# A hybrid encoder block in fp32: gate and value as one loop over both halves of the tokens, operands loaded later in program order, made operands in the ring of the sums

## The chip, the cores and the metric

One core of one Trainium2 chip. The time is the device time of one execution in microseconds (us); lower is better. TensorE is PE in the profile (its weight loads PEld), VectorE is DVE, ScalarE is ACT, GpSimd is POOL, SyncE is SP. SPq and ACTq are the DMA issues in the instruction streams of SP and ACT.

## The reference

One layer on 2048 tokens of width 1024 with a feed-forward width of 2816. Everything is fp32. The change lies in `conv_ffn`.

```python
def reference(x, ...):
    h = rmsnorm(x, mix_norm_w[i])
    y = gla_mixer(h, gla_w_in, gla_w_gate2, gla_b_gate, gla_norm_w, gla_w_out)
    x = x + y
    h = rmsnorm(x, ffn_norm_w[i])
    x = x + conv_ffn(h, w_up, conv_w, conv_b, w_down)
    return rmsnorm(x, final_norm_w)

def conv_ffn(h, w_up, conv_w, conv_b, w_down):
    u = causal_dwconv(h @ w_up, conv_w, conv_b)   # 3 taps along the tokens
    g, val = jnp.split(u, 2, axis=-1)
    return (jax.nn.silu(g) * val) @ w_down
```

## The kernel before, in words

The mixer's projections run as four passes (R, A, B, Y). The feed-forward then has two parts: gate and value (`phase_u`, h @ w_up with convolution, Silu and product) and down (w_down). A fp32 product is made of three matmuls on split numbers: `split` writes a rounded copy (ACT, the CAST of L184) and the rest (DVE, the TENSOR_TENSOR of L185).

**Products.** Each large matrix product is done by a seven-product scheme on 2 by 2 blocks: `OPS` names the seven products p1, p5, p6, p7, p4, p2, p3 in the order in which they run. A product is 12 matmuls of 128x512 (4 slices of the inner dimension, 3 matmuls each, L177 to L179) into a PSUM bank. p1, p6, p7 and p4 add up in one bank (`ua`), p5 and p3 in another (`uc`), p2 has its own (`ub`). Between them ACT copies the bank out: after p1 (c1, L1052), after p6 (c2, L1052), after p7 (c3, L1143) and after p4 (L1150). The next product into that bank has to wait for the copy.

**Gate and value before.** `phase_u(s)` runs once for each half s of the tokens (1024 each). In it 22 column blocks f go in 11 groups of two; a group is 14 products (seven for each of its two f). In each half there are therefore 154 products. For each group:
- `load` brings raw blocks of w_up (`ur`, 256 KB a DMA, on SP) into a ring of four; those for the next group are asked for at products 2 and 7 of this one.
- `prep` makes and splits the weight operand of a product (`uw_p`), five products ahead (`ULEAD`); POOL makes the sums (`us`).
- `conv` and `gated` turn u into the gated product t; POOL makes four sums of it (`as_p`, a ring of four 2 KB tiles that c3 shares), and SP stores them to DRAM (`ad_p<-as_p`) with the products themselves (`ad_p<-t`).

**Operands of the tokens.** The token side of each of the seven products stays in SBUF for a whole half (`h_p`, 2 MB each, tile `uh`). It is made once by `prep_h2` (split into `h2p_p`), stored to DRAM (`hd_p`), and brought back by `load_op` in four DMAs of 512 KB on SP. For the second half the 28 operands (7 products times 4 pairs of token tiles) are made while the first half of gate and value runs: `spread` calls one step about every 11 us of planned PE time; it loads rows (`h2r`) on SP, subtracts (L791), splits, and stores through ACT's queue (L786). Before, the tile `h2p` for this has a single buffer of 4 KB a partition (hi and lo together) in the pool `wx`.

**What sets the order.** The instructions of each engine run in the order of the program. That order comes from the order of the calls, from the planned clock (`later_do` delays a call by a planned time), and from a scheduler that moves instructions ahead on an engine where it takes them to be ready. An engine, SP and ACT as DMA issuers too, stops at the first instruction that must wait.

**Between the halves before.** The loop of s = 0 ends; only then does `phase_u(1)` ask for its first raw blocks and make its first weights. The seven `load_op` of the second half stand right behind the last use of the same operand of the first half.

**Last tiles of h.** `x1_done` normalises a tile of 128 tokens, and `blocks` transposes it on PE (`pt_d`, L755) NLY = 5.5 us of planned time later. For the last two tiles (14, 15) this falls among the first products of gate and value.

Of the kernel before, what the change touches and what calls it, by code (L numbers as in the profile page):

```python
# [16 lines left out]
P = 128  # L17
# [8 lines left out]
def hybrid_kernel(  # L26
# [36 lines left out]
    WB = 4  # L63
    WX = 3
    HB = 4
    RB = 4
# [3 lines left out]
    DLY, KLY, XLY = 5.0, 2.0, 6.5  # L70
    NLY = 5.5
    Y0, Y1, U0, U1 = 3.0, 2.8, 14.0, 11.0
# [667 lines left out]
    def x1_done(t, xt):  # L740
        if "p" not in yp:
            y_open()
        (nc.scalar if t + 2 >= NTT else nc.sync).dma_start(x1d[t], xt)
        rws = yp["p"].tile([P, D], F32, tag="rows", name=f"h2_{t}", bufs=2)
        rstd = rstd_of(xt, D, f"d{t}", rws, "a")
        nc.scalar.activation(rws, xt, AF.Identity, scale=rstd)
        later_do(NLY, lambda: blocks(t, rws))

# [20 lines left out]
    def prep_h2(jj, raw, pair):  # L769
# [13 lines left out]
        def store():  # L783
            while held:
                o, hl = held.pop()
                (nc.scalar if s else nc.sync).dma_start(hd[s, o, j], f32(hl))  # L786
# [77 lines left out]
    def unit(ps_, j):  # L864
# [28 lines left out]
        for i, o in enumerate(PORD):  # L893
# [31 lines left out]
            if j + 1 == NP:  # L925
                if nxt:
                    if i == 0:
                        plan_w(nxt)
                else:
                    if i == 0:  # L930
                        need(*(f"h2p{jj}" for jj in range(PAIRS)))
                    load_op(0, o)
                    if i == 3:
                        ux["u"] = phase_u(0)
                        next(ux["u"])
# [72 lines left out]

    def phase_u(s):
        raws, wops, sums, made = {}, {}, {}, {}  # L1010
        jobs = [(g, o, f) for g in range(NQ) for o in OPS for f in (2 * g, 2 * g + 1)]


        def load(g, n):
            for f in (2 * g, 2 * g + 1):
# [6 lines left out]
        def prep(k):  # L1022
            g, o, f = jobs[k]
            a11, a21 = raws[f, 0][:, 0, :], raws[f, 0][:, 1, :]
# [29 lines left out]

        def new_u(i, f):
            c = f + i * NF
# [4 lines left out]

        def conv(i, f):
            c = f + i * NF
# [10 lines left out]

        def gated(f):
            t, v = made.pop(("t", 0, f)), made.pop(("t", 1, f))
# [26 lines left out]
        bank = {}  # L1103
        for k, (g, o, f) in enumerate(jobs):
            if k % (2 * len(OPS)) in (2, 7) and g + 1 < NQ:
                load(g + 1, int(k % (2 * len(OPS)) == 7))
            if s == 0 and k == 6:
                while delayed:
# [3 lines left out]
                pools["us"] = pools["ctx"].enter_context(tc.tile_pool(name="us", bufs=1, reuse_waits="tile"))  # L1112
                pools["wx"] = wx_ = pools["ctx"].enter_context(tc.tile_pool(name="wx", bufs=1, reuse_waits="tile"))
                spread(range(PAIRS, 2 * PAIRS), U0, U1, row_tile,
                       lambda name: wx_.tile([P, 2, 512], F32R, tag="h2p", name=name, bufs=1))
            if s == NS - 1 and g == NQ - 1 and f % 2 == 0:
# [17 lines left out]
            elif o == "p2":  # L1134
                pb = mm_ps(f"ub_{s}_{f}")
                mm3p(pb, pairs)
                ev, _ = new_u(0, f)
                nc.vector.tensor_add(ev, tiles1(pb), tiles1(made.pop(("p1", f))))
            elif o == "p7":
                a = bank["a", f]  # L1140
                mm3p(a, pairs, first=False, more=True)
                u3 = pools["us"].tile([P, 512], F32, tag="as", name=f"c3_{s}_{f}", bufs=4)
                nc.scalar.copy(u3, a)  # L1143
                ev, od = new_u(1, f)
                made["ev", f] = ev
                nc.vector.tensor_add(od, tiles1(bank["c", f]), tiles1(u3))
            elif o == "p4":
                a = bank.pop(("a", f))
                mm3p(a, pairs, first=False, more=True)
                nc.scalar.copy(made.pop(("ev", f)), tiles1(a))  # L1150
                conv(1, f)
# [6 lines left out]
            if o == "p3":  # L1158
                _, od = tiles2(made["u", 0, f][:, 2:2 + TS])
                nc.vector.tensor_add(od, tiles1(c), tiles1(made.pop(("u2", f))))  # L1160
                conv(0, f)
                gated(f)

# [232 lines left out]
```

## Time and profile before

| | |
|---|---|
| median of 3 runs | 2259.55 us (2251.75 to 2259.7) |
| the profiled execution: time, span | 2255.93 us, 2254.2 us |
| gate and value, first half (11 groups) | 909.81 to 1373.58 us of the span |
| gate and value, second half (11 groups) | 1373.58 to 1822.53 us |
| PE busy over the span | 2125.4 us, 94% |
| DVE, ACT, POOL busy | 71%, 49%, 32% |

In the views a row of the timeline is: start, duration, engine, line, operation, out<-in, shape, count, and in brackets the idle time of the engine just before it with what ended it. A row of a table of stretches is: from:to, length, then busy time and number of instructions of PE, PEld, DVE, ACT and POOL, the granted TensorE clock (1.00 is full), the DMA share and GB/s.

### The profile page before, as it was taken

Reading aid. Unit: us, or ns where it says so; the run is one execution under the profiler, and the core shown is the slowest. Engines: PE = TensorE matmul, PEld = TensorE weight load, DVE = VectorE, ACT = ScalarE, POOL = GpSimd, SP = SyncE. Lnnn points to the kernel's source line nnn. Section 1 sums busy time; section 2 is a strip of 40 time slices with the busy share of each in tenths; the row PEclk is TensorE's granted clock in tenths of the full one; section 3 lists DMA queues with packets and bytes.
Section 4 is the critical chain, followed back from the end, with each engine's and each line's share of the span. In section 5 each row is a group of like instructions: output and inputs, shape, how many; then the busy total and the mean of one; then the engine's idle time right before and its main releaser. Section 6 shows DMA issues by size and latency. Waiting matters only on the chain.

```text
span 2254.2 us, 29125 instructions
## 1 busy us (share of the span) xinstructions
PE 2125.4 (94%) x9948; PEld 1738.4 (77%) x9948; DVE 1609.5 (71%) x2175; ACT 1111.0 (49%) x2020; POOL 712.1 (32%) x602
## 2 busy tenths in 40 slices
PE   5999989989998999989999996999999999999998
PEld 4788778877886787767777884888888887888886
DVE  7755787788778675488898774786767776557464
ACT  4554655565556676444554452554544543232342
POOL 1000111111111000355555663555555534036100
PEclk9999999999999999999999997999999999999999
DMA  6545683368557799935544248324242468354443
GB/s 209 197 165 180 209 289 122 122 213 314 164 159 235 250 328 337 334 126 191 178 145 146 83 126 308 108 80 131 71 138 72 131 239 309 129 188 153 140 168 117
DMA packets 301045, 411.77 MB, mean 183 GB/s; under 512 B 23246, under 2 KB 159614, under 8 KB 300896
## 3 DMA queue, kind: packets, MB, share of 16 engines
q1 hardware_dynamic: 266156, 346.72, 46.1%
q10 hardware_dynamic: 34740, 63.19, 8.2%
q8 instruction: 78, 1.28, 0.2%
q14 instruction: 71, 0.58, 0.1%
HBM read 266.70 MB, written 143.13 MB: 182 GB/s over the span
## 4 chain that ended last, share of the span: by engine, by line
PE 67%; DVE 12%; DMA 9%; issue 5%; ACT 4%; POOL 3%; ACTq 0%; SPq 0%; DVEq 0%; POOLq 0%
PE ua L177 5%; PE ua L178 5%; PE ua L179 5%; PE pd_p L178 5%; PE pd_p L177 5%; PE pd_p L179 5%; PE uc L178 3%; PE uc L179 3%; PE uc L177 3%; DVE t L1070 2%; PE mp_R L177 2%; PE mp_R L178 2%; PE mp_R L179 2%; PE mp_Y L177 2%; PE mp_Y L178 2%
## 5 line engine op out<-in xcount | busy, mean ns | idle before, releaser
L177 PE MATMUL ua<-h_p,uw_p 128*128 128x512 f32 x704 | 281.2, 399 | 45.3 <-ACT uw_p L184 22.0
L178 PE MATMUL ua<-h_p,uw_p 128*128 128x512 f32 x704 | 279.2, 397 | 0.0
L179 PE MATMUL ua<-h_p,uw_p 128*128 128x512 f32 x704 | 278.5, 396 | 0.0
L1070 DVE SCALAR_TENSOR_TENSOR t<-u,cw,t 128x1024 f32<-128x1024 f32 x176 | 249.9, 1424 | 11.2 <-ACT t L1068 9.7
L178 PE MATMUL pd_p<-dw_p,da 128*128 128x512 f32 x616 | 240.5, 390 | 1.9 <-DVE da L185 1.9
L177 PE MATMUL pd_p<-dw_p,da 128*128 128x512 f32 x616 | 240.4, 390 | 0.0
L179 PE MATMUL pd_p<-dw_p,da 128*128 128x512 f32 x616 | 240.3, 390 | 0.0
L185 DVE TENSOR_TENSOR uw_p<-ur,uw_p 128x512 fp32r<-128x512 f32 x176 | 159.4, 920 | 84.7 <-ACT uw_p L184 71.2
L185 DVE TENSOR_TENSOR da<-da_p,da 128x512 fp32r<-128x512 f32 x154 | 131.9, 910 | 102.3 <-ACT da L184 102.2
L177 PEld LDWEIGHTS ua<-h_p,uw_p 128*128 128x128 f32 x704 | 134.2, 191 | 81.3 <-ACT c L1052 26.5
L184 ACT CAST da<-da_p 128x512 fp32r<-128x512 f32 x154 | 85.1, 619 | 204.5 <-PE pd_p L179 148.7
L185 DVE TENSOR_TENSOR uw_p<-us,uw_p 128x512 fp32r<-128x512 f32 x132 | 119.1, 910 | 63.3 <-ACT uw_p L184 56.5
L179 PEld LDWEIGHTS ua<-h_p,uw_p 128*128 128x128 f32 x704 | 134.3, 191 | 30.1
L178 PEld LDWEIGHTS ua<-h_p,uw_p 128*128 128x128 f32 x704 | 134.3, 191 | 29.6 <-DVE uw_p L185 0.4
L184 ACT CAST uw_p<-us 128x512 fp32r<-128x512 f32 x132 | 82.1, 622 | 126.7 <-POOL us L1032 74.2
L177 PE MATMUL uc<-h_p,uw_p 128*128 128x512 f32 x352 | 138.2, 393 | 0.0
L178 PE MATMUL uc<-h_p,uw_p 128*128 128x512 f32 x352 | 138.1, 392 | 0.0
L179 PE MATMUL uc<-h_p,uw_p 128*128 128x512 f32 x352 | 138.0, 392 | 0.0
L1068 ACT ACTIVATE t<-u,cw 128x1024 f32<-128x1024 f32 x88 | 109.7, 1247 | 57.0 <-DVE u L1160 56.8
L178 PEld LDWEIGHTS pd_p<-dw_p,da 128*128 128x128 f32 x616 | 116.1, 188 | 26.7 <-DVE da L185 2.8
L179 PEld LDWEIGHTS pd_p<-dw_p,da 128*128 128x128 f32 x616 | 116.0, 188 | 24.3
L177 PEld LDWEIGHTS pd_p<-dw_p,da 128*128 128x128 f32 x616 | 116.0, 188 | 24.2
(251 smaller groups left out, 5441.6 us busy)
## 6 DMA issues: line engine op xcount, KB each, us to landing
ur<-in_ffn_w_up_dram SPq DMA_DIRECT2D x168, 256.0 KB, 3.5
da_p<-ad_p SPq DMA_DIRECT2D x154, 256.0 KB, 3.8
h_p<-hd_p SPq DMA_DIRECT2D x56, 512.0 KB, 9.2
ad_p<-as_p SPq DMA_DIRECT2D x88, 256.0 KB, 2.3
ad_p<-t SPq DMA_DIRECT2D x66, 256.0 KB, 3.0
x<-in_x_dram SPq DMA_DIRECT2D x32, 512.0 KB, 5.1
ch<-in_ffn_w_down_dram SPq DMA_DIRECT2D x61, 256.0 KB, 4.3
hr_A_p<-h1d_p SPq DMA_DIRECT2D x56, 256.0 KB, 2.9
```

The lines of the kernel that those rows point to most:

```text
L177: nc.tensor.matmul(ps_ap, ah, bl, start=(first and i == 0), stop=False, **kw)
L178: nc.tensor.matmul(ps_ap, al, bh, start=False, stop=False, **kw)
L179: nc.tensor.matmul(ps_ap, ah, bh, start=False, stop=(last and i == len(pairs) - 1), **kw)
L184: nc.scalar.copy(hi, src)
L185: nc.vector.tensor_sub(lo, src, f32(hi))
L1068: nc.scalar.activation(t, u[:, 2:2 + TS], AF.Identity, scale=cw[:, 2, c:c + 1], bias=cw[:, 3, c:c + 1])
L1070: nc.vector.scalar_tensor_tensor(t, u[:, k:k + TS], cw[:, k, c:c + 1], t, op0=ALU.mult, op1=ALU.add)
```

## The change

1. `phase_u` becomes one loop over (s, group, product, f). Loads and `prep` run across the border of the halves as across any border of two groups.
2. `load_op` of the second half is called three products after the last use of the operand instead of right behind it.
3. The 28 made operands no longer have a tile of their own: hi and lo each take a tile of 2 KB from the ring `as`, which grows from 4 to 6 buffers (SBUF use is the same). Each is stored by two DMAs of 256 KB instead of one of 512 KB; where more than one store is held back, the oldest goes first.
4. The transposes of tiles 14 and 15 are called after 9.0 us of planned time (`NLE`) instead of 5.5.

```diff
+    AB = 6
...
-    NLY = 5.5
+    NLY, NLE = 5.5, 9.0
...
-        later_do(NLY, lambda: blocks(t, rws))
+        later_do(NLY if t + 2 < NTT else NLE, lambda: blocks(t, rws))
...
         def store():
             while held:
-                o, hl = held.pop()
-                (nc.scalar if s else nc.sync).dma_start(hd[s, o, j], f32(hl))
+                o, hl = held.pop(0)
+                if s == 0:
+                    nc.sync.dma_start(hd[s, o, j], f32(hl))
+                else:
+                    for i in range(2):
+                        nc.scalar.dma_start(hd[s, o, j][:, i, :], f32(hl[i]))
...
             hl = pair(f"h2p_{jj}_{o}")
-            split(hl[:, 0, :], hl[:, 1, :], ts[n])
+            hi, lo = hl if s else (hl[:, 0, :], hl[:, 1, :])
+            split(hi, lo, ts[n])
...
-    def phase_u(s):
+    def phase_u():
         raws, wops, sums, made = {}, {}, {}, {}
-        jobs = [(g, o, f) for g in range(NQ) for o in OPS for f in (2 * g, 2 * g + 1)]
+        jobs = [(s, g, o, f) for s in range(NS) for g in range(NQ) for o in OPS for f in (2 * g, 2 * g + 1)]
+        GJ = 2 * len(OPS)
...
-                t = pools["us"].tile([P, 512], F32, tag="as", name=f"as_{s}_{q}_{o}", bufs=4)
+                t = pools["us"].tile([P, 512], F32, tag="as", name=f"as_{s}_{q}_{o}", bufs=AB)
...
-        for k, (g, o, f) in enumerate(jobs):
-            if k % (2 * len(OPS)) in (2, 7) and g + 1 < NQ:
-                load(g + 1, int(k % (2 * len(OPS)) == 7))
-            if s == 0 and k == 6:
+        for k, (s, g, o, f) in enumerate(jobs):
+            if k % GJ in (2, 7) and k // GJ + 1 < NS * NQ:
+                load(k // GJ + 1, int(k % GJ == 7))
+            if k > 3:
+                ls, lg, lo_, lf = jobs[k - 3]
+                if ls + 1 < NS and lg == NQ - 1 and lf % 2 == 1:
+                    need(*(f"h2p{jj}" for jj in range(PAIRS, 2 * PAIRS)))
+                    load_op(ls + 1, lo_)
+            if k == 6:
...
-                       lambda name: wx_.tile([P, 2, 512], F32R, tag="h2p", name=name, bufs=1))
+                       lambda name: tuple(pools["us"].tile([P, 512], F32R, tag="as", name=f"{name}_{i}", bufs=AB) for i in range(2)))
...
-                u3 = pools["us"].tile([P, 512], F32, tag="as", name=f"c3_{s}_{f}", bufs=4)
+                u3 = pools["us"].tile([P, 512], F32, tag="as", name=f"c3_{s}_{f}", bufs=AB)
...
-            if s + 1 < NS and g == NQ - 1 and f % 2 == 1:
-                need(*(f"h2p{jj}" for jj in range(PAIRS, 2 * PAIRS)))
-                load_op(s + 1, o)
...
-    for s in range(NS):
-        for _ in ux.get("u") or phase_u(s):
-            pass
-        ux.clear()
+    for _ in ux["u"]:
+        pass
```

**How the rows move.** Three places. The numbers in a name are half, block f or group, and product; the last number only tells buffers apart. `ur_1_0_0` is half 1, f 0, first raw block.

First, SP at the border of the halves (L848, in the new file L854, is `load_op`; L1019 / L1027 the raw blocks; L1081 to L1097 / L1089 to L1105 the stores of the gated product and its sums). Before, behind the operand of p3:

```order
L848 DMA h_1_p3_13206<-hd_1_p3_3_341 128x2x512
L1084 DMA ad_0_p2_10_407<-t_0_21_13213 512x1x128
L1085 DMA ad_0_p4_10_396<-t_0_21_13213 512x1x128
L1097 DMA ad_0_p5_10_363<-as_0_10_p5_13221 128x512
L1097 DMA ad_0_p6_10_374<-as_0_10_p6_13224 128x512
L1097 DMA ad_0_p3_10_418<-as_0_10_p3_13227 128x512
L1097 DMA ad_0_p7_10_385<-as_0_10_p7_13230 128x512
L1019 DMA ur_1_1_0_13236<-in_ffn_w_up_dram 128x4x128 x2
L1019 DMA ur_1_0_1_13239<-in_ffn_w_up_dram 128x4x128 x2
```

The raw blocks of f 1 (`ur_1_1_0`) and the second ones of f 0 and f 1 stand behind the last sums of the first half. The same queue after the change, one group earlier:

```order
L1027 DMA ur_1_0_0_13021<-in_ffn_w_up_dram 128x4x128 x2
L1089 DMA ad_0_p1_9_351<-t_0_18_12936 512x1x128
L854 DMA h_1_p1_13060<-hd_1_p1_0_314 128x2x512
L1027 DMA ur_1_1_0_13024<-in_ffn_w_up_dram 128x4x128 x2
L1092 DMA ad_0_p2_9_406<-t_0_19_12962 512x1x128
L1093 DMA ad_0_p4_9_395<-t_0_19_12962 512x1x128
```

`ur_1_1_0` has moved ahead of the sums of group 9; `ur_1_0_1` and `ur_1_1_1` follow the operand of p5. What moved back instead are the operands of p2 and p3, behind the last sums of the first half and with raw blocks between them:

```order
L1105 DMA ad_0_p7_10_385<-as_0_10_p7_13309 128x512
L854 DMA h_1_p2_13312<-hd_1_p2_0_334 128x2x512
L854 DMA h_1_p2_13312<-hd_1_p2_1_335 128x2x512
L854 DMA h_1_p2_13312<-hd_1_p2_2_336 128x2x512
L854 DMA h_1_p2_13312<-hd_1_p2_3_337 128x2x512
L1027 DMA ur_1_2_0_13356<-in_ffn_w_up_dram 128x4x128 x2
L1027 DMA ur_1_3_0_13359<-in_ffn_w_up_dram 128x4x128 x2
L854 DMA h_1_p3_13362<-hd_1_p3_0_338 128x2x512
```

Second, ACT in group 1 of the first half, where the made operands p5 and p7 of pair 4 are cast and stored ahead of the copies c2. Before:

```order
L786 DMA hd_1_p5_0_318<-h2p_4_p5_10089 128x1024
L184 CAST uw_0_2_p2_10135<-ur_0_2_1_9852 128x512
L184 CAST h2p_4_p7_10162<-h2r_4_1_9950 128x512
L786 DMA hd_1_p7_0_326<-h2p_4_p7_10162 128x1024
L1052 COPY c2_0_2_10133<-ua_0_2_10040 128x512
L184 CAST uw_0_3_p2_10152<-ur_0_3_1_9855 128x512
L1052 COPY c2_0_3_10150<-ua_0_3_10059 128x512
```

After:

```order
L185 CAST h2p_4_p5_0_10091<-h2r_4_0_9948 128x512
L791 DMA hd_1_p5_0_318<-h2p_4_p5_0_10091 128x512
L791 DMA hd_1_p5_0_318<-h2p_4_p5_1_10092 128x512
L1060 COPY c2_0_2_10137<-ua_0_2_10042 128x512
L185 CAST uw_0_3_p2_10156<-ur_0_3_1_9855 128x512
L185 CAST h2p_4_p7_0_10166<-h2r_4_1_9950 128x512
L791 DMA hd_1_p7_0_326<-h2p_4_p7_0_10166 128x512
L791 DMA hd_1_p7_0_326<-h2p_4_p7_1_10167 128x512
L1060 COPY c2_0_3_10154<-ua_0_3_10061 128x512
```

The operands come later (one step of p5 instead of p7 ahead of c2 of f 2), the two stores stand right behind the cast, and the second of them still stands ahead of c2. Over the whole half the casts of made operands by group were 2, 6, 6, 8, 6 (each up to the eighth copy of a group) and are 1, 5, 3, 5, 4, 4, 4, 2.

Third, PE among the first products, where the transposes of tile 14 stand. Before:

```order
L178 MATMUL ua_0_1_9679<-h_0_p1_9486,uw_0_1_p1_9651 128x512
L179 MATMUL ua_0_1_9679<-h_0_p1_9486,uw_0_1_p1_9651 128x512
L755 MATMUL pt_d14_0_9683<-ident_496,h2_14_9613 128x128 x4
L755 MATMUL pt_d14_1_9694<-ident_496,h2_14_9613 128x128 x4
L177 MATMUL ua_0_1_9679<-h_0_p1_9486,uw_0_1_p1_9651 128x512
```

After:

```order
L179 MATMUL uc_0_0_9705<-h_0_p5_9510,uw_0_0_p5_9656 128x512
L180 MATMUL uc_0_0_9705<-h_0_p5_9510,uw_0_0_p5_9656 128x512
L756 MATMUL pt_d14_0_9712<-ident_496,h2_14_9613 128x128 x4
L756 MATMUL pt_d14_1_9723<-ident_496,h2_14_9613 128x128 x4
L178 MATMUL uc_0_0_9705<-h_0_p5_9510,uw_0_0_p5_9656 128x512
```

They stand 15 matmuls later, in the middle of the first p5 instead of the second p1.

More of the change, by code (lines that the diff above doesn't have):

```diff
@@ L933, in unit @@
                     if i == 3:
-                        ux["u"] = phase_u(0)
+                        ux["u"] = phase_u()
                         next(ux["u"])
@@ L1007, in hybrid_kernel, with load @@
     wuv = w_up.rearrange("(kt p) c -> p kt c", p=P)
-    def phase_u(s):
+    def phase_u():
         raws, wops, sums, made = {}, {}, {}, {}
-        jobs = [(g, o, f) for g in range(NQ) for o in OPS for f in (2 * g, 2 * g + 1)]
-        def load(g, n):
+        jobs = [(s, g, o, f) for s in range(NS) for g in range(NQ) for o in OPS for f in (2 * g, 2 * g + 1)]
+        GJ = 2 * len(OPS)
+        def load(sg, n):
+            s, g = divmod(sg, NQ)
             for f in (2 * g, 2 * g + 1):
@@ L1022, in prep @@
         def prep(k):
-            g, o, f = jobs[k]
+            s, g, o, f = jobs[k]
             a11, a21 = raws[f, 0][:, 0, :], raws[f, 0][:, 1, :]
@@ L1053, in copied, with new_u @@
             return t
-        def new_u(i, f):
+        def new_u(s, i, f):
             c = f + i * NF
@@ L1060, in new_u, with conv @@
             return tiles2(u[:, 2:2 + TS])
-        def conv(i, f):
+        def conv(s, i, f):
             c = f + i * NF
@@ L1073, in conv, with gated @@
             made["t", i, f] = t
-        def gated(f):
+        def gated(s, f):
             t, v = made.pop(("t", 0, f)), made.pop(("t", 1, f))
@@ L1112, in phase_u @@
                 pools["us"] = pools["ctx"].enter_context(tc.tile_pool(name="us", bufs=1, reuse_waits="tile"))
-                pools["wx"] = wx_ = pools["ctx"].enter_context(tc.tile_pool(name="wx", bufs=1, reuse_waits="tile"))
+                pools["wx"] = pools["ctx"].enter_context(tc.tile_pool(name="wx", bufs=1, reuse_waits="tile"))
                 spread(range(PAIRS, 2 * PAIRS), U0, U1, row_tile,
-                       lambda name: wx_.tile([P, 2, 512], F32R, tag="h2p", name=name, bufs=1))
+                       lambda name: tuple(pools["us"].tile([P, 512], F32R, tag="as", name=f"{name}_{i}", bufs=AB) for i in range(2)))
             if s == NS - 1 and g == NQ - 1 and f % 2 == 0:
@@ L1136, in phase_u @@
                 mm3p(pb, pairs)
-                ev, _ = new_u(0, f)
+                ev, _ = new_u(s, 0, f)
                 nc.vector.tensor_add(ev, tiles1(pb), tiles1(made.pop(("p1", f))))
@@ L1150, in phase_u @@
                 nc.scalar.copy(made.pop(("ev", f)), tiles1(a))
-                conv(1, f)
+                conv(s, 1, f)
             else:
```

7 lines of the change are left out of this document (3 added, 4 removed).

## The prediction

> **What bounds the kernel now.** I read the page's engine shares first, then a table of stretches cut at the starts of the groups of gate and value, then timeline rows around each idle time of PE, then the waits of the tile `h2p_p`.
>
> ```profile
> PE 2125.4 (94%) x9948; PEld 1738.4 (77%) x9948; DVE 1609.5 (71%) x2175; ACT 1111.0 (49%) x2020; POOL 712.1 (32%) x602
> ```
>
> PE is the bound; the other engines matter where they make it wait. The stretches are group 0, group 1, groups 2 to 6, groups 7 to 10 of the first half, then group 0 and groups 1 to 10 of the second:
>
> ```profile
> core 0: us, PE busy (x) PEld busy (x) DVE busy (x) ACT busy (x) POOL busy (x), PEclk, DMA share, GB/s
> 909.81:955.84 46.03, 43.06 (x186) 35.30 (x185) 20.40 (x26) 23.18 (x46) 17.09 (x18) 0.93 0.97 345
> 955.84:1006.62 50.78, 41.26 (x170) 32.99 (x169) 41.74 (x40) 22.66 (x36) 28.90 (x25) 0.90 0.39 129
> 1006.62:1219.34 212.72, 198.98 (x841) 158.61 (x840) 186.47 (x188) 107.72 (x164) 122.65 (x102) 0.98 0.49 162
> 1219.34:1373.58 154.24, 154.24 (x673) 126.05 (x672) 112.67 (x117) 73.28 (x108) 85.69 (x74) 1.00 0.45 145
> 1373.58:1436.93 63.35, 41.32 (x170) 32.98 (x168) 34.29 (x35) 21.97 (x33) 30.62 (x24) 0.81 0.58 192
> 1436.93:1822.53 385.60, 385.60 (x1682) 315.14 (x1680) 285.61 (x303) 193.43 (x290) 208.74 (x155) 1.00 0.38 117
> ```
>
> A group without a stall is 154.24 / 4 = 385.60 / 10 = 38.56 us, so a product is 38.56 / 14 = 2.75 us. Above that stand: group 0 7.47, group 1 12.22, groups 2 to 6 together 212.72 - 192.80 = 19.92, groups 7 to 10 nothing, second half's group 0 24.79, the rest nothing. The change can touch only these 64.4 us, less the transposes in group 0, which are work. The last column but two tells that the throttle took part: 0.81 where PE stood longest.
>
> **The change: the border (parts 1 and 2).**
>
> ```profile
> 1353.00 23.79 SPq L848 DMA_DIRECT2D h_p<-hd_p  x22
> ...
> 1376.07 0.39 PE L179 MATMUL ua<-h_p,uw_p 128*128 128x512 f32 x1
> ...
> 1379.40 4.49 SPq L848 DMA_DIRECT2D h_p<-hd_p  x4
> ...
> 1387.08 3.96 SPq L1097 DMA_DIRECT2D ad_p<-as_p  x4
> ...
> 1391.64 24.85 SPq L1019 DMA_DIRECT2D ur<-in_ffn_w_up_dram  x14
> ...
> 1397.82 0.62 ACT L184 CAST uw_p<-ur 128x512 fp32r<-128x512 f32 x1 [16.82 <-DMA ur<-in_ffn_w_up_dram]
> ...
> 1398.49 0.79 PE L177 MATMUL ua<-h_p,uw_p 128*128 128x512 f32 x1 [22.03 <-ACT uw_p L184]
> ...
> 1403.78 0.39 PE L177 MATMUL uc<-h_p,uw_p 128*128 128x512 f32 x1
> ```
>
> PE ends p1 of f 0 at 1376.46 and stands 22.03 us for the weight of f 1, whose raw block SP issued only at 1391.64, behind the operands and the last sums. The 12 matmuls of p1 of f 1 then take 1403.78 - 1398.49 = 5.29 instead of 2.75 us: 2.5 us of slow clock. 22.0 + 2.5 make up the 24.8. After the change that raw block stands a group earlier on SP and the second raw blocks behind the operand of p5, so this wait goes whole. What is late next: the operands of p2 and p3, now behind the last sums. PE wants p2 ten products into the group, 1373.58 + 27.5 = 1401.1, and p3 at 1406.6. SP is free of the sums at 1387.08 + 3.96 = 1391.0. At the 345 GB/s of group 0, the stretch that loads most, 2.1 MB take 6.1 us and the 1 MB of raw blocks between them 3.0: p2 is there at 1397.1, p3 at 1391.0 + 6.1 + 3.0 + 6.1 = 1406.2, plus the issue's own way to landing, which at 2 us (the sums' 2.3 below) makes p3 about 2 us late. I take 24.8 - 2 = **-22.8**. Ends: all 24.8; or 24.8 less one median landing of an operand (9.2, below), 15.6. The 28 operand issues themselves stay 28, and the split weights of the border stay as many; ACT and DVE do them while PE works through group 10, which shows no stall.
>
> **The made operands (part 3).** The waits at the tile: idle before it, then who waited for it (us, times).
>
> ```profile
>   DMA hd_p<-h2p_p: 34.8, 23
>   ACT h2p_p L184: 14.0, 13
> ...
>   ACT c L1052: 12.2, 6
> ```
>
> With one buffer each cast waits until the store before it has landed: 34.8 / 23 = 1.5 us of ACT a time. Then the store's issue waits for DVE's subtraction, and the copy c2 behind it waits with it. In group 1:
>
> ```profile
> 972.85 0.33 ACTq L786 DMA_DIRECT2D hd_p<-h2p_p  x1
> ...
> 977.18 0.62 ACT L184 CAST h2p_p<-h2r 128x512 fp32r<-128x512 f32 x1 [3.29 <-DMA hd_p<-h2p_p]
> ...
> 979.46 1.75 DVE L185 TENSOR_TENSOR h2p_p<-h2r,h2p_p 128x512 fp32r<-128x512 f32 x1
> ...
> 981.60 0.58 ACT L1052 COPY c<-ua 128x512 f32<-128x512 f32 x1 [3.80 <-DVE h2p_p L185]
> ...
> 982.24 0.80 PE L177 MATMUL ua<-h_p,uw_p 128*128 128x512 f32 x1 [8.35 <-ACT c L1052]
> ```
>
> and in groups 3 to 5, with two stretches around such stalls:
>
> ```profile
> 1067.42 0.50 PE L177 MATMUL ua<-h_p,uw_p 128*128 128x512 f32 x1 [2.94 <-ACT c L1052]
> ...
> 1115.81 0.50 PE L177 MATMUL ua<-h_p,uw_p 128*128 128x512 f32 x1 [2.56 <-ACT c L1052]
> ...
> 1159.08 0.50 PE L177 MATMUL ua<-h_p,uw_p 128*128 128x512 f32 x1 [2.61 <-ACT c L1052]
> ```
>
> ```profile
> 1106.00:1122.00 16.00, 12.64 (x47) 9.53 (x46) 11.54 (x11) 5.25 (x11) 10.38 (x7) 0.89 0.91 292
> 1152.00:1168.00 16.00, 13.01 (x55) 9.79 (x54) 12.49 (x14) 8.26 (x15) 11.30 (x9) 1.00 0.76 255
> ```
>
> After the change a cast no longer waits for the store just ahead of it, but for the tile six back in the ring, which may be a sum whose store is out. In an undisturbed group (from 1335.02) that comes at
>
> ```profile
> 1346.15 1.67 POOL L1091 TENSOR_TENSOR as_p<-t,t 128x512 f32<-128x512 f32 x1 [1.18 <-DVE t L1077]
> ...
> 1347.85 5.09 SPq L1097 DMA_DIRECT2D ad_p<-as_p  x4
> 1348.91 0.59 ACT L1052 COPY c<-ua 128x512 f32<-128x512 f32 x1 [2.13 <-PE ua L179]
> ```
>
> ```profile
> h_p<-hd_p SPq DMA_DIRECT2D x56, 512.0 KB, 9.2
> ...
> ad_p<-as_p SPq DMA_DIRECT2D x88, 256.0 KB, 2.3
> ...
> hd_p<-h2p_p ACTq DMA_DIRECT2D x28, 512.0 KB, 3.3
> ```
>
> 1347.85 + 2.3 = 1350.2, some 1.2 us after c2 could have begun (1348.91): where a made operand hits this place, a wait of that size stays. The wait of the store for DVE stays too, with c2 behind it. So of a stall of 2.7 us (mean of the three) I take off the 1.5 of the landing and keep 1.2, one a group, in five groups: 6.0 of the 19.9, **-14**. Ends: nothing (DVE, 186.47 of 212.72 or 88% here, is late either way) and all 19.9. The 28 extra issues at 0.33 us are 9.2 us of ACT, which is 107.72 of 212.72 us busy, so I cost them at nothing; if ACT's cover fails just ahead of c2, it is 0.33 a step.
>
> The Trainium skill ("TensorE: Matmul & The Clock Gate", Part 1) says that the clock halves after an idle window of about 3.4 us, counted in free-running windows. The stretch around the 2.56 us stall shows 0.89 and that around 2.61 shows 1.00, so shorter stalls sometimes pay here and the rule's threshold is not sharp; by the rule alone these groups' stalls would be their idle time and the sum would come out less by about 2 us.
>
> **Transposes (part 4) and groups 0, 1.**
>
> ```profile
> 915.14 1.15 ACT L746 ACTIVATE h<-x,rstd_d 128x1024 f32<-128x1024 f32 x1 [2.93 <-POOL rstd_d L207]
> 916.34 1.97 PE L755 MATMUL pt_d<-ident,h 128*128 128x128 f32 x8 [2.97 <-ACT h L746]
> ...
> 936.21 11.02 SPq L1019 DMA_DIRECT2D ur<-in_ffn_w_up_dram  x8
> ...
> 949.51 1.75 POOL L1029 TENSOR_TENSOR us<-ur,ur 128x512 f32<-128x512 f32 x1
> ```
>
> h is ready at 916.29; PE came at 913.37. Fifteen matmuls of 2.75 / 12 = 0.23 us later it comes at 916.8 and waits for nothing: 2.97 us gone there. But the raw blocks of group 1 are issued at 936.21 to 947.23 behind a DMA share of 0.97 and their sum starts at 949.51, whatever PE does; what PE gains before, it waits there. I keep a quarter, 0.7. In group 1 the 3.29 of the landing goes from the 8.35: **-4.0** in all. Ends: -1 (DVE late) and 2.97 + 8.35 = -11.3.
>
> **Sum.** 22.8 + 14 + 4 = 40.8, against the profiled execution's 2255.93 us: 2215.1, so 2215. That execution lies 3.6 below the median of the runs (2259.55) and 4.2 above the lowest.
>
> **Rivals.** One: DVE takes the ring's place. The copies wait for the subtraction, not for the landing; DVE's 88% and the 3.80 at c2 speak for it, against it that the steps are spread over eight groups instead of five. The middle part gives 3, groups 0 and 1 give 1: 22.8 + 3 + 1 = 26.8, 2229.
>
> Two: p2 and p3 come late at the border. With the median landing, p2 is there at 1391.0 + 4.5 (issue of four) + 9.2 = 1404.7, 3.6 late, p3 3.6 more behind raw blocks, and 2.5 of slow clock: the border gives 24.8 - 9.7 = 15, the sum 33, 2223. For it speaks the 9.2; against it that this median is of loads queued 22 in a row.
>
> Three: every stall goes. 24.8 + 19.9 + 11.3 = 56, 2200. Groups 7 to 10 run without any at the same work less the made operands; against it stands the wait for DVE.
>
> Four, slower: the second store of each step holds ACT. If each of the 28 extra stores cost PE a landing of 2.3 us, because the next cast waits in the ring for it, that is +64.4 - 22.8 - 4, 2293; it decides from 26.8 / 28 = 0.96 us a step. The ring of six holds three steps and ACT is half idle, which speaks against it. The Trainium skill ("DMA: Bandwidth & Descriptors", "Anatomy of one DMA") gives each DMA about 2.0 us that do not depend on size, against splitting a store; the rows, 3.3 us for 512 KB and 2.3 for 256 KB, agree, and by its figure the 28 would be 56 us if paid in line.
>
> Five: the border's wait is only exchanged, PE stands for p3 as long as for the raw block, and the middle gains little: about 2250.
>
> **How the numbers follow.** Forecast 0.50, one 0.20, two 0.13, three 0.11, four 0.03, five 0.03. The likeliest time is 2215. The best ends of the parts give 2200, the worst 15.6 + 3 + 1 = 19.6, 2236 (with the middle part at rival one's value, not at its end of nothing). Execution to execution adds about 4: 2195 to 2240, which leaves out four, five and a tail. 0.5% is 11 us, about what a measurement of this kernel can tell from no change: faster 0.94, same 0.03 (five), slower 0.03 (four).
>
> **What would show it.** Border: no idle time of PE over 5 us after the first p1 of the second half, its group 0 at 38.6 to 42 us; a wait of the p2 or p3 matmuls on `h_p` is rival two. Ring: no idle time of ACT on the store of `h2p_p` right before a cast, groups 2 to 8 within 6 us of 38.56 each in sum; copies c2 waiting on DVE in most groups is rival one, casts waiting on `hd_p` is four. Transposes: no idle time before `pt_d` of tile 14, and group 1's start little earlier. I am wrong if the groups with made operands grow: DVE or the ring then set the pace in eight groups instead of five.

## The result and the profile after

| | before | after |
|---|---|---|
| median of 4 runs | 2259.19 us (2251.75 to 2259.7) | 2239.68 us (2236.85 to 2241.21) |
| the profiled execution, span | 2254.2 us | 2238.9 us |

The ratio is 0.992 [0.9896, 0.9943]: faster by 19.5 us, a little under half of the 40.8 that were forecast. The table of stretches of the changed kernel, cut at its own group starts (groups 0; 1; 2 to 6; 7 to 10; of these group 8 alone; then group 0 and groups 1 to 10 of the second half; columns as before):

```profile
core 0: us, PE busy (x) PEld busy (x) DVE busy (x) ACT busy (x) POOL busy (x), PEclk, DMA share, GB/s
914.74:963.55 48.81, 42.48 (x186) 34.17 (x184) 19.95 (x27) 23.18 (x46) 18.58 (x19) 0.97 0.90 310
963.55:1010.55 47.00, 41.65 (x170) 33.29 (x168) 38.48 (x39) 20.77 (x32) 27.19 (x23) 0.93 0.40 129
1010.55:1211.08 200.53, 193.88 (x842) 157.38 (x840) 184.04 (x175) 102.18 (x156) 124.92 (x101) 1.00 0.48 152
1211.08:1378.02 166.94, 159.28 (x674) 129.10 (x672) 132.30 (x132) 78.95 (x119) 95.69 (x79) 0.97 0.51 162
1250.35:1297.05 46.70, 41.58 (x170) 33.51 (x169) 34.84 (x36) 20.11 (x31) 25.68 (x22) 0.93 0.41 124
1378.02:1424.45 46.43, 41.58 (x171) 33.24 (x170) 30.51 (x31) 18.75 (x28) 22.26 (x19) 0.93 0.78 257
1424.45:1809.82 385.37, 385.37 (x1681) 315.19 (x1679) 308.77 (x304) 194.91 (x293) 219.81 (x159) 1.00 0.38 117
```

Set against the rows of before, stage by stage (us):

| stage | before | after | forecast | measured |
|---|---|---|---|---|
| up to gate and value | 909.81 | 914.74 | 0 | +4.9 |
| groups 0 and 1 | 96.81 | 95.81 | -4 | -1.0 |
| groups 2 to 6 | 212.72 | 200.53 | -14 | -12.2 |
| groups 7 to 10 | 154.24 | 166.94 | 0 | +12.7 |
| second half | 448.95 | 431.80 | -22.8 | -17.2 |
| down to the end | 431.67 | 429.08 | 0 | -2.6 |
| span | 2254.2 | 2238.9 | -40.8 | -15.3 |

The first row is not the change's: up to the transposes of tile 14 every engine has the same instructions in the same order in both kernels, and over the executions profiled below this start lies between 909.8 and 919.2. What is left, -20.2, agrees with the medians. The last stage lies between 427.4 and 432.7 over the same executions, so its -2.6 is not shown to be the change's either. The two that matter: what groups 2 to 6 gave, groups 7 to 10 took back, and the border gave three quarters of its term.

The larger idle times of PE after the change, with what ended them:

```profile
939.81 0.50 PE L178 MATMUL ua<-h_p,uw_p 128*128 128x512 f32 x1 [4.68 <-ACT c L1060]
...
985.80 0.79 PE L178 MATMUL ua<-h_p,uw_p 128*128 128x512 f32 x1 [4.98 <-ACT c L1060]
...
1029.73 0.50 PE L178 MATMUL ua<-h_p,uw_p 128*128 128x512 f32 x1 [2.54 <-ACT c L1060]
...
1071.26 0.50 PE L178 MATMUL ua<-h_p,uw_p 128*128 128x512 f32 x1 [2.70 <-ACT c L1060]
...
1272.10 0.79 PE L178 MATMUL ua<-h_p,uw_p 128*128 128x512 f32 x1 [5.12 <-ACT c L1060]
...
1315.79 0.80 PE L178 MATMUL ua<-h_p,uw_p 128*128 128x512 f32 x1 [2.10 <-ACT c L1060]
...
1409.75 0.77 PE L178 MATMUL ub<-h_p,uw_p 128*128 128x512 f32 x1 [4.13 <-DMA h_p<-hd_p]
...
1418.77 0.48 PE L178 MATMUL uc<-h_p,uw_p 128*128 128x512 f32 x1 [0.72 <-DMA h_p<-hd_p]
```

One stall each in groups 0, 1, 2, 3, 8 and 9, all on a copy of ACT, and two at the border on the operands of p2 and p3. Groups 4 to 7 and 10 have none over 0.8 us. The four groups 2, 3, 8 and 9 (41.36, 41.53, 46.70, 42.41) carry 17.8 us above 38.56 each. Group 8 shows the mechanism, in the timeline of ACT, POOL and SP:

```profile
1264.08 0.62 ACT L185 CAST h2p_p<-h2r 128x512 fp32r<-128x512 f32 x1
...
1264.73 2.86 ACTq L791 DMA_DIRECT2D hd_p<-h2p_p  x2
...
1265.01 1.68 POOL L1099 TENSOR_TENSOR as_p<-t,t 128x512 f32<-128x512 f32 x1 [1.19 <-DVE t L1085]
...
1266.71 4.88 SPq L1105 DMA_DIRECT2D ad_p<-as_p  x4
...
1270.95 0.62 ACT L185 CAST h2p_p<-h2r 128x512 fp32r<-128x512 f32 x1 [5.73 <-DMA ad_p<-as_p]
1271.47 0.58 ACT L1060 COPY c<-ua 128x512 f32<-128x512 f32 x1
```

The second cast takes the ring tile of this group's first sum. POOL makes that sum at 1265.01, SP issues its store at 1266.71, the cast starts 4.2 us later, and c2 stands behind the cast. By the order of ACT's instructions just four casts wait for the first sum of the group they stand in and stand ahead of both copies c2: one in each of groups 2, 3, 8 and 9. In the trace these four stand 5.5 to 5.7 us each, and no other cast of a made operand over 0.8. The waits at the tile (idle before it; then who waited):

```profile
  DMA ad_p<-as_p: 15.0, 4
  DMA hd_p<-h2p_p: 11.5, 7
...
  ACT c L1060: 15.4, 8
```

The old wait for the store's landing came down from 34.8 us (23 times) to 11.5 (7), as forecast; the wait of 15.0 in 4 for a sum's store is new. Only two of these four are casts (groups 2 and 8, 11.4 us); the others are subtractions on DVE. For the casts of groups 3 and 9 the brackets name another release:

```profile
1070.10 0.62 ACT L185 CAST h2p_p<-h2r 128x512 fp32r<-128x512 f32 x1 [5.46 <-DVE h2r L796]
...
1314.64 0.62 ACT L185 CAST h2p_p<-h2r 128x512 fp32r<-128x512 f32 x1 [5.48 <-DMA hd_p<-h2p_p]
```

The first sum's store had landed 0.4 and 0.3 us before (issued at 1066.12 and 1310.65, landed 3.6 and 3.7 us later), and DVE's subtraction for the cast (L796) ended 0.1 us before each. So the place of the cast is the same in all four, but in two of them DVE was as late as the sum's store.

### The profile page after: what moved, and what is told of

Its sections match the earlier page's. It is cut to its first block, busy times and chain, and to the rows that moved or that the text cites. A ratio compares the mean times of both kernels' runs of the same rounds, so it can differ in the third digit from the quotient of the medians.

```text
span 2238.9 us, 29122 instructions
## 1 busy us (share of the span) xinstructions
PE 2126.9 (95%) x9948; PEld 1741.8 (78%) x9948; DVE 1642.1 (73%) x2175; ACT 1107.5 (49%) x2020; POOL 729.1 (33%) x602
## 4 chain that ended last, share of the span: by engine, by line
PE 62%; DVE 14%; DMA 9%; issue 5%; ACT 5%; POOL 3%; SPq 1%; ACTq 0%; DVEq 0%; POOLq 0%
PE pd_p L179 5%; PE pd_p L180 5%; PE pd_p L178 5%; PE ua L178 5%; PE ua L179 5%; PE ua L180 5%; DVE t L1078 4%; PE mp_R L178 2%; PE uc L178 2%; PE uc L180 2%; PE uc L179 2%; PE mp_R L179 2%; PE mp_R L180 2%; DVE uw_p L186 2%; PE mp_A L178 1%
## 5 line engine op out<-in xcount | busy, mean ns | idle before, releaser
L1078 DVE SCALAR_TENSOR_TENSOR t<-u,cw,t 128x1024 f32<-128x1024 f32 x176 | 264.2, 1505 | 8.6 <-ACT t L1076 7.5
L186 DVE TENSOR_TENSOR uw_p<-ur,uw_p 128x512 fp32r<-128x512 f32 x176 | 168.4, 973 | 59.4 <-ACT uw_p L185 52.3
L178 PEld LDWEIGHTS ua<-h_p,uw_p 128*128 128x128 f32 x704 | 134.3, 191 | 58.1 <-ACT c L1060 28.6
L1076 ACT ACTIVATE t<-u,cw 128x1024 f32<-128x1024 f32 x88 | 109.7, 1247 | 50.9 <-DVE u L1169 43.0
```

Of the source, the lines that this page charges most:

```text
L178: nc.tensor.matmul(ps_ap, ah, bl, start=(first and i == 0), stop=False, **kw)
L186: nc.vector.tensor_sub(lo, src, f32(hi))
L1076: nc.scalar.activation(t, u[:, 2:2 + TS], AF.Identity, scale=cw[:, 2, c:c + 1], bias=cw[:, 3, c:c + 1])
L1078: nc.vector.scalar_tensor_tensor(t, u[:, k:k + TS], cw[:, k, c:c + 1], t, op0=ALU.mult, op1=ALU.add)
```

## The experiments

All times in us. The stages are read from the group starts of each profiled execution; the ratio is against the kernel before on the same chip.

| kernel | groups 0, 1 | 2 to 6 | 7 to 10 | second half | median | ratio [interval] |
|---|---|---|---|---|---|---|
| before | 96.8 | 212.7 | 154.2 | 449.0 | 2259.2 | |
| after | 95.8 | 200.5 | 166.9 | 431.8 | 2239.7 | 0.992 [0.9896, 0.9943] |
| e1 transposes back | 94.0 | 202.0 | 167.6 | 431.9 | 2242.1 | 0.9916 [0.99, 0.9933] |
| e2 own tile | 97.1 | 212.9 | 154.2 | 432.1 | 2245.0 | 0.9939 [0.9915, 0.9963] |
| e3 lag one | 93.9 | 201.9 | 163.5 | 430.5 | 2239.5 | 0.991 [0.9894, 0.9925] |
| e4 steps at products | 90.2 | 194.4 | 154.2 | 436.6 | 2221.5 | 0.9829 [0.9815, 0.9844] |
| f1 p2, p3 by ACT | 96.2 | 199.7 | 166.3 | 429.1 | 2239.8 | 0.9916 [0.9896, 0.9935] |
| f2 seven waits | 98.1 | 207.5 | 160.3 | 432.7 | 2243.0 | 0.9934 [0.9918, 0.9951] |
| f3 own tile at products | 94.8 | 213.6 | 154.2 | 432.3 | 2237.5 | 0.9905 [0.9885, 0.9924] |
| f4 at products, p2, p3 by ACT | 86.5 | 193.9 | 154.2 | 433.4 | 2214.4 | 0.9803 [0.9785, 0.9821] |
| g1 all operands by ACT | 89.8 | 193.7 | 159.2 | 438.2 | 2228.2 | 0.9865 [0.9843, 0.9887] |
| g2 as f4, transposes back | 87.5 | 194.3 | 154.3 | 432.9 | 2216.0 | 0.9809 [0.9794, 0.9824] |
| h1 as f4, lag four | 92.4 | 193.7 | 154.3 | 434.3 | 2215.4 | 0.9798 [0.9782, 0.9815] |
| i1 as e4, lag four | 89.2 | 194.9 | 154.4 | 432.5 | 2219.1 | 0.9829 [0.9809, 0.9849] |

### Where the ring's gain went

**Part 3 undone** (e2).

```diff
-    AB = 6
+    AB = 4
-        lambda name: tuple(pools["us"].tile([P, 512], F32R, tag="as", name=f"{name}_{i}", bufs=AB) for i in range(2))
+        lambda name: pools["wx"].tile([P, 2, 512], F32R, tag="h2p", name=name, bufs=1)
```

> Part 3 undone (one tile of its own for made operands, ring of four). Theory: the ring moved the waits more than it removed them. Groups 2 to 6 go back up by about 12 us to 213, groups 7 to 10 come down by about 12.7 to 154.2, group 1 goes up by 3; the time is 2240 to 2244. Rival, as predicted: the ring is worth 14 us in itself, and the time is 2253.

Groups 2 to 6 went back to 212.9 and groups 7 to 10 to 154.2, 12.4 up and 12.7 down: the theory holds stage by stage. The median, 2245.0, stands 1 over the expected 2240 to 2244 and 5 over the changed kernel's; the two intervals overlap, and the stages of gate and value together differ by 1.3.

**The steps called at products** (e4).

```diff
+            if s == 0 and k > 6 and k % GJ in (7, 9, 11, 13):
+                made["go"]()
```

(`go` makes one step; the planned time between steps is gone.)

> The steps that make the operands of the second half are called at fixed products (7, 9, 11 and 13 of each group) instead of by planned time; on ACT no cast of a made operand then stands between the stores of the sums of the same group and the copies c2. All else as after the change. Theory: the stalls of groups 2, 3, 8 and 9 come from the cast that waits for the landing of the first sum's store with c2 behind it; their excess of 17.8 us falls to 4 or less and the time to 2226. Rival: the copies wait for DVE's subtraction wherever the steps stand; the casts now come in bursts and c1 or c3 waits as much as c2 did; the excess stays over 12 us and the time at 2236 to 2240.

Groups 2 to 10 as one stretch, then group 0 of the second half:

```profile
1005.53:1354.13 348.60, 347.70 (x1513) 283.31 (x1512) 326.79 (x303) 179.46 (x273) 221.88 (x176) 1.00 0.49 156
1354.13:1405.38 51.25, 43.55 (x170) 34.43 (x169) 32.37 (x33) 19.73 (x30) 26.72 (x23) 0.90 0.83 278
```

348.60 is 9 x 38.56 = 347.04 and 1.6: no stall over 0.6 us is left, with as much work on DVE (326.79 of 348.60, 94% busy), and no cast of a made operand has more than 0.4 us of idle ACT ahead of it. So DVE's load alone did not hold PE, nor did the ring by itself; what held it was a cast that has to wait, standing ahead of c2. With the order of after the change and a larger ring no kernel was run, so how long these casts would wait for DVE alone stays open. Group 1 came down too, from 47.0 to 41.4. The rival falls. The border went up by 4.8, which comes below.

**Seven such places instead of four** (f2): `U1` 11.0 to 10.0.

> As after the change, with the planned time between two steps at 10.0 instead of 11.0 us. By the order of ACT's instructions seven casts (groups 2 to 8) instead of four (2, 3, 8, 9) then wait for the first sum's store of the same group with c2 behind them. Theory: each is worth 17.8 / 4 = 4.4 us; three more make the first half 13 us longer, the stalls stand in groups 2 to 8, the time is 2250 to 2253. Rival: the number of such places says nothing, since DVE's load decides; the steps are a little denser and end earlier, and the time stays at 2236 to 2243.

PE's idle time, first and last of the seven:

```profile
1028.29 0.50 PE L178 MATMUL ua<-h_p,uw_p 128*128 128x512 f32 x1 [1.85 <-ACT c L1060]
...
1278.32 0.50 PE L178 MATMUL ua<-h_p,uw_p 128*128 128x512 f32 x1 [1.66 <-ACT c L1060]
```

The stalls stand in groups 2 to 8, one each, as the order said, and group 9 has none. But groups 2 to 10 hold 207.5 + 160.3 - 347.0 = 20.8 us of stalls, 3.0 a place and not 4.4, and grew by 0.3 us against the changed kernel (367.5) instead of by 13. The place is right, a constant price a place is wrong. Each of the seven casts waits 5.1 to 5.5 us, much as the four did:

```profile
1027.13 0.62 ACT L185 CAST h2p_p<-h2r 128x512 fp32r<-128x512 f32 x1 [5.49 <-DMA hd_p<-h2p_p]
```

What differs is how late in its group the cast starts: 16.9 to 18.6 us here, with 1.40 to 3.16 us of idle PE, and 17.6 to 20.6 after the change, with 2.10 to 5.12. In all eleven places PE's idle time is that start less 15.5; what comes on top, 0.3 to 3.0 us, is slower work of PE. The brackets name the made operand's own store in six of the seven and DVE's subtraction in one, never the sum's store. The median, 2243.0, lies on the upper edge of the rival's 2236 to 2243.

**Own tile, with the steps at products** (f3): part 3 undone as in e2, the calls as in e4.

> Part 3 undone (one tile of its own), and the steps called at products 7, 9, 11 and 13 of each group as in the faster of the kernels before. In the order of ACT's instructions casts and stores still stand ahead of copies c1 and c2 in groups 1 to 6, five a group, each behind its own store's landing. Theory: place alone does not do it, a cast with the wait in front of the copies costs as with the tile of its own before; groups 1 to 6 stay over their 231 us by 20 or more and the time at 2240 to 2246. Rival: with the calls at these products the ring is not needed; groups 2 to 10 lose their stalls and the time is 2222 to 2226.

Groups 2 to 6 kept 213.6 and the time was 2237.5, below the 2240 to 2246 expected but 16 above e4. With one tile casts and stores stand ahead of the copies in this order too; the ring lets them stand elsewhere. It is worth 16 us where they do; in the order that the change gave them, the 5 us between the medians are not clear of the spread.

### The border

**Lag one** (e3): `jobs[k - 3]` to `jobs[k - 1]`.

> Operands of the second half loaded one product behind the last use instead of three; on SP the operand of p2 then stands ahead of the last sums of the first half and that of p3 right behind them, without raw blocks between. Theory: the 4.85 us that PE waits for p2 and p3 and the slow clock after it go; the second half of gate and value takes 424 to 426 us instead of 431.8, the time is 2232. Rival: the operands that come earlier on SP hold the raw blocks of f 0 and f 1, PE waits for a weight instead, the second half stays at 430 to 432 and the time at 2240.

PE no longer waits for p2 or p3. But ACT and PE show, in group 0 of the second half,

```profile
1396.44 1.06 ACT L1080 ACTIVATE t<-t 128x1024 f32<-128x1024 f32 x1 [2.80 <-DVE t L1078]
...
1398.54 0.80 PE L178 MATMUL ua<-h_p,uw_p 128*128 128x512 f32 x1 [2.84 <-ACT c L1060]
```

a copy behind an activation that waits for DVE. The second half fell by 1.3 of the 7 expected: the rival holds, in that a copy takes the operands' place.

**p2 and p3 issued by ACT** (f1), and the same on e4 (f4):

```diff
-            nc.sync.dma_start(f32(t[:, :, j, :]), hd[s, o, j])
+            (nc.scalar if s and o in ("p2", "p3") else nc.sync).dma_start(f32(t[:, :, j, :]), hd[s, o, j])
```

> The operands of p2 and p3 of the second half are issued in ACT's stream instead of SP's, three products behind the last use as after the change; all else as after the change. Theory: p2 and p3 come late because SP reaches them only behind the last sums (1394.97 to 1400.4 us), not because the DMA engines are full; the waits of 4.13 and 0.72 us and the slow clock go, the second half of gate and value takes 424 to 426 us, the time is 2233. Rival: the DMA engines are the limit at the border (share over 1.0, 350 to 390 GB/s); the earlier operands take from the raw blocks, a copy or a weight comes late, and the second half stays at 430 to 432, the time at 2239.

> Steps at products 7, 9, 11 and 13 (ring of six), and the operands of p2 and p3 of the second half in ACT's stream. Theory: the waits of PE for p2 and p3 (2.45 and 1.44 us) go, the wait for the copy of p1 (3.82) stays; the second half goes from 436.6 to 431 or 432 us, the time from 2221.5 to 2217. Rival: the earlier operands hold the raw blocks longer, the copy comes later still, and the second half stays at 436 or more, the time at 2222.

In f1 the waits for p2 and p3 went and a copy's wait of 2.59 us came: 429.1, between the two theories, with no gain in the median. In f4 the second half came to 433.4, 3.3 less than in e4 and short of the 431 expected. The median, 2214.4, is 7.1 below e4's; in the profiled executions 3.7 of the difference lies in groups 0 and 1, where both kernels have the same order on every engine, so not all of the 7.1 is shown to be the edit's. With h1 and g2 it is the fastest kernel run, and faster than before and after.

**All 28 operand loads by ACT** (g1): `nc.scalar if s else nc.sync`.

> Steps at products 7, 9, 11 and 13 (ring of six), and all 28 operand loads of the second half in ACT's stream, so that on SP the second raw blocks of f 0 and f 1 stand right behind the sums of group 9. Theory: at the border the copy of p1 is late because the second raw blocks are issued behind operands on SP, so the sums on POOL and the splits on DVE run late; issued at once behind the sums, about 6 us earlier, the wait of 3.37 us and its slow clock go, the second half takes 425 to 428 us instead of 433.4, the time is 2207 to 2209. Rival: the DMA engines are full at the border (share over 1.0), so operands and raw blocks only exchange places: PE waits for an operand or still for the copy, the second half stays at 432 to 435 and the time at 2214.

Neither came: 438.2, and group 10 of the first half now stalls as well (43.5). SP issues the second raw blocks at 1331.00, 22 us ahead of the second half (1353.45), where f4 has 11, so they did come earlier. ACT stands instead, at an operand's issue with c2 behind it:

```profile
1331.23 0.53 ACTq L857 DMA_DIRECT2D h_p<-hd_p  x1
1331.80 0.58 ACT L1063 COPY c<-ua 128x512 f32<-128x512 f32 x1 [6.88 <-DMA ad_p<-t]
```

The issue waited for a transfer of SP's: the store `ad_p<-t` issued at 1323.43 landed 7.8 us later, at 1331.2, and had the semaphore that this issue uses (last section). The next two move the raw blocks by the lag instead.

**Lag four**, with p2 and p3 by ACT (h1) and with all on SP (i1): `jobs[k - 3]` to `jobs[k - 4]`.

> As the fastest of the kernels before (steps at products 7, 9, 11 and 13, the operands of p2 and p3 in ACT's stream), with the operands loaded four products behind the last use instead of three. On SP the second raw blocks of f 0 and f 1 then stand ahead of the operand of p5 instead of behind it. Theory: the copy of p1 is late at the border since the raw blocks come late; 2 MB earlier, they come some 5 us sooner, the wait of 3.37 us and its slow clock shrink, the second half takes 427 to 430 us instead of 433.4, the time is 2208 to 2211. Rival: POOL and DVE are late there by their own load (the gated product and the sums of the last group), not by the raw blocks; the wait stays, the second half is 432 to 435, the time 2214.

> Steps at products 7, 9, 11 and 13, all operand loads in SP's stream, four products behind the last use instead of three: the second raw blocks of f 0 and f 1 stand ahead of the operand of p5, and no operand load is issued by ACT. Theory: in the kernel with the same lag and ACT's stream the copies were held by ACT's own DMA issues; without these the earlier raw blocks alone act: the wait of PE for the copy of p1 (3.82 us with lag three) falls below 1 us, the waits for p2 and p3 (2.45 and 1.44) stay, the second half takes 430 to 434 us instead of 436.6, the time is 2216 to 2219. Rival: POOL and DVE are late at the border by their own load; the wait for the copy stays over 3 us and the second half at 436 or more, the time at 2221 to 2224.

ACT and PE in h1:

```profile
1368.96 6.02 ACTq L857 DMA_DIRECT2D h_p<-hd_p  x3
1375.03 1.14 ACT L185 CAST uw_p<-ur 128x512 fp32r<-128x512 f32 x2 [8.09 <-issue]
...
1376.70 0.79 PE L178 MATMUL ua<-h_p,uw_p 128*128 128x512 f32 x1 [7.16 <-ACT c L1063]
```

The waits for the copy of p1 shrank to 0.30 and 0.42 us, but ACT's stream stood between two of the three issues (last section) and c2 waited behind them: 434.3 instead of 427 to 430. That is inside the rival's range, but not for the rival's reason. In i1, without them, POOL starts the sum of the first raw blocks at 1343.12, 7.8 us ahead of the second half (1350.90), where e4 has 1352.45 for 1354.13:

```profile
1343.12 1.28 POOL L1040 TENSOR_TENSOR us<-ur,ur 128x512 f32<-128x512 f32 x1 [9.29 <-DMA ur<-in_ffn_w_up_dram]
...
1383.36 0.77 PE L178 MATMUL ub<-h_p,uw_p 128*128 128x512 f32 x1 [4.78 <-DMA h_p<-hd_p]
```

No wait for a copy is left at the border and p2's is back: 432.5, inside the 430 to 434. So the raw blocks' place decides the copy's wait and the sums on SP decide p2's. The one order run here with little of either, h1, pays 7.16 us at c2 instead.

### The transposes

**Part 4 undone** (e1 on the changed kernel, g2 on f4): `NLE` 9.0 to 5.5.

> Part 4 undone (transposes of tiles 14 and 15 at 5.5 us again). Theory: in group 0 ACT waits for the landing of the store of the transposed h (3.97 and 3.88 us after the change) wherever the transposes stand, and the copy of p1 behind it holds PE; groups 0 and 1 together stay at 95.8 us within 3, the time at 2240 within 5. Rival: the later place itself causes the 4.68 us stall of group 0; then groups 0 and 1 together come down by 3 to 5 us to about 91 to 93, the time to 2236.

> Steps at products 7, 9, 11 and 13, the operands of p2 and p3 in ACT's stream, and part 4 undone (transposes of tiles 14 and 15 at 5.5 us of planned time again). Theory: part 4 costs a little in group 0, where the copies of h hold ACT for the landing of their stores with the copy of p1 behind them; groups 0 and 1 come to 84 to 88 us, the time to 2212 to 2215. Rival, as predicted: the earlier transposes wait 3 us for h and part 4 is worth 1 to 4 us; groups 0 and 1 come to 88 to 91 us, the time to 2216 to 2218.

Groups 0 and 1 differ by -1.9 (e1) and +1.0 (g2), the medians by +2.4 and +1.6, all within the spread of executions: groups 0 and 1 alone read 86.5 to 92.4 in the five kernels with the steps at products (e4, f4, g1, h1, i1), which have the same order there. Part 4 exchanges one stall for another. In g2 PE waits for h:

```profile
923.66 1.97 PE L756 MATMUL pt_d<-ident,h 128*128 128x128 f32 x8 [3.65 <-ACT h L747]
```

After the change it doesn't. But ACT waits for the store of the transposed tile, with the copy behind it:

```profile
932.05 1.14 ACT L760 ACTIVATE hb<-pt_d,nw 128x128 f32<-128x128 f32 x4 [3.97 <-DMA h2f<-hb]
...
939.17 0.58 ACT L1060 COPY c<-ua 128x512 f32<-128x512 f32 x1 [3.88 <-DMA h2f<-hb]
```

That copy is the one PE waits 4.68 us for at 939.81. ACT's wait isn't new; before the change the same copy has it:

```profile
932.85 0.59 ACT L1052 COPY c<-ua 128x512 f32<-128x512 f32 x1 [3.38 <-DMA h2f<-hb]
```

There, and in e1, PE comes later, since it has stood for h, and has no wait for this copy; in g2 it is 0.81 us. Whether part 4 is worth a microsecond either way stays open.

## Why the prediction was right and wrong

**Right.** The 22.03 us for the raw block went whole, and what came late next were the operands of p2 and p3, as said. The landing wait at the tile fell to a third. In group 1 the 3.29 us of the landing was to go, and the group came from 50.78 to 47.00. The extra stores cost next to nothing on PE as stores (rival four): in e4, with two stores a step, PE stands 0.9 us in groups 2 to 10. By the difference of the two rows that rival four names, 3.3 - 2.3 us for 256 KB more, the part of a store that does not depend on its size would be 1.3 us, an estimate; 2.0 is not what they show.

**Wrong: the made operands.** The step that failed is "where a made operand hits this place, a wait of that size stays", sized 1.2 us from group 10, and with it the 0 for groups 7 to 10. The place was named rightly. Its size in group 8: c2 starts at 1271.47, while p6 of the first f ended five products into the group, at 1250.35 + 5 x 2.75 = 1264.1; it is 7.3 us late. Group 10 of before has no made operands on DVE; there the first sum started 11.1 us into the group (1346.15 - 1335.02), in group 8 at 14.7 (1265.01 - 1250.35), and from its store's issue to the cast passed 4.2 us instead of 2.3. Of the 12.7, 5.0 are work of PE at a slower clock (159.28 us busy instead of 154.24), which the term left out. And the change spread the steps over groups that had run free: two of the four bad places are in groups 8 and 9, 8.14 + 3.85 = 12.0 of the 12.7 given back. "The change can touch only these 64.4 us" missed that. So did the count by group ahead of the prediction, five groups before and eight after: in the traces the casts run in groups 0 to 6 before (1, 5, 5, 4, 6, 5, 2) and in groups 0 to 9 after (1, 3, 3, 4, 3, 3, 3, 3, 3, 2). "One a group, in five groups" could have been counted from the order instead: four places, two outside the five groups. That groups 2 to 6 came to -12.2, near the -14, is in part luck: two stalls of 2.5 and 2.7 us and little else are left there, not five of 1.2. The forecast's own sign of error ("I am wrong if the groups with made operands grow") is what came. DVE's load alone is not the reason, which e4 shows, but in two of the four places its subtraction was as late as the store.

**Wrong by a size: the border.** -22.8 came to -17.2. The step is "SP is free of the sums at 1391.0": it was read from a border at which PE stood and DVE had little to do. POOL and the stretch, before:

```profile
1382.34 1.26 POOL L1091 TENSOR_TENSOR as_p<-t,t 128x512 f32<-128x512 f32 x1 [2.09 <-DVE t L1077]
```

```profile
1373.58:1390.00 16.42, 2.88 (x13) 2.06 (x11) 7.38 (x7) 3.78 (x4) 6.48 (x7) 0.68 1.05 388
```

and after, with SP's issues:

```profile
1393.27 1.67 POOL L1099 TENSOR_TENSOR as_p<-t,t 128x512 f32<-128x512 f32 x1 [1.19 <-DVE t L1085]
...
1394.97 5.44 SPq L1105 DMA_DIRECT2D ad_p<-as_p  x4
1400.50 2.55 SPq L854 DMA_DIRECT2D h_p<-hd_p  x4
```

```profile
1378.02:1395.00 16.98, 16.98 (x76) 13.91 (x75) 15.00 (x16) 10.69 (x16) 11.32 (x10) 1.00 0.70 250
```

The sums begin 8.8 us into the group before and 15.3 after, with DVE busy 15.00 of 16.98 instead of 7.38 of 16.42. SP reaches p2 at 1400.5, 22.5 us into the group instead of the 17.4 assumed. PE wants it at 27.5, and 22.5 with the 6.1 us of 2.1 MB is 28.6, before any way to landing; the last operand of p2 is there at 31.7. The forecast left 2 us of loss here. What came is 4.85 us of waits (4.13 and 0.72) and 3.0 of slower work of PE (41.58 us busy instead of 38.56), for which it had nothing. Rival two, 15, came nearer than the forecast, and its sign, a wait of p2 and p3 on `h_p`, came. That its time for p2, 31.1 us into the group, is so near is luck: it has SP free 5.1 us too early and too long a way to landing. e4 shows the same once more: the first half lost 24.5 us of stalls (463.3 to 438.8), and the border paid 4.8 of it back, its second raw blocks and sums now nearer to the start of the second half.

**Wrong: the transposes.** "It comes at 916.8 and waits for nothing" is right for PE; the term missed that the transposed tile comes from the copies' ring, so that a copy of ACT waits for its store's landing, wherever the transposes stand. What PE gains at h it can lose at that copy: group 0 came from 46.03 to 48.81, within the 45.5 to 50.9 of the five kernels with the same order. With group 1 the -4 came to -1.0.

## What to carry to other kernels

A buffer shared with another stream moves a wait to that stream's last step: look in the order for the instruction that will wait, and for what an in-order engine holds behind it, and count those places. When a stall goes, due times read from beside it (who is early, when a queue is free) go with it: take them from a stretch where PE runs. Where steps are spread thinner, cost the groups that were free before. Where a DMA is to be issued by an engine with due work, ask which earlier transfer its issue will wait for.

## What was not expected of the hardware

Three DMA issues of ACT stand in one row of 6.02 us in h1, in a stretch with the DMA engines full (share 1.06, 387 GB/s):

```profile
1368.00:1376.00 8.00, 1.54 (x7) 0.92 (x5) 0.66 (x2) 0.97 (x2) 5.23 (x4) 0.82 1.06 387
```

The issues themselves take 0.5 to 0.6 us each. After the first ACT's stream stands 4.3 us, and the other two follow:

```profile
1373.79 1.20 ACTq L857 DMA_DIRECT2D h_p<-hd_p  x2
```

The second begins 0.03 us after the landing, at 1373.76, of a load that SP had issued at 1363.57. Both use the same semaphore to tell of their landing. In this trace all DMAs of the program, SP's and ACT's, share eight semaphores (169 or 170 issues each), and this issue waits on its own until the load that used it before has landed. Here such a landing takes 10.2 us, and ACT's later work waits with the issue. In g1 it is the same, with a store of SP's and 7.8 us. No kernel with semaphores of its own for ACT was run.

Slow matmuls after a stall don't go by its length alone. The granted clock over the 4 us after the 2.10 us stall that ended at 1315.79, and after the 2.70 that ended at 1071.26:

```profile
1315.79:1319.79 4.00, 4.00 (x11) 3.20 (x12) 1.83 (x3) 1.57 (x3) 0.00 (x0) 0.59 0.94 283
1071.26:1075.26 4.00, 4.00 (x17) 3.30 (x18) 3.31 (x6) 2.47 (x5) 0.00 (x0) 1.00 0.92 269
```

The Trainium skill ("TensorE: Matmul & The Clock Gate", Part 1) ties the slow clock to an idle, free-running window of about 3.4 us; the first of these rows is against it as a threshold.
